# A rope table loaded one token group earlier: the order of groups in attention's last v part

## The chip, the core and the metric

The kernel runs on one core of a Trainium2 chip. The metric is the device time of one execution in microseconds (us). The engines named below are PE (TensorE, matrix products), DVE (VectorE), ACT (ScalarE), POOL (GpSimd) and SP, whose instruction queue issues the transfers. Each engine works through its own instructions strictly in order and waits on semaphores for the others.

## What is computed

One mixer layer over 1024 latent tokens with 256 context tokens in front, all in float32. A normalised and modulated input `h` (latent) or `hc` (context) goes through one wide projection. Branch A is a bidirectional chunked gated DeltaNet with 8 heads; branch B is differential softmax attention with 8 heads of two 64-wide halves. Both are gated, projected, merged and added to `x`. For the change only the preparation of branch B matters:

```
q_l = diff_heads(q_b, q_norm_w, rope)      # latent tokens: RMS norm of each 64, gain, 2-D rope
k_l = diff_heads(k_b, k_norm_w, rope)
k_c = diff_heads(k_bc, k_norm_w, None)     # context tokens: no rope, and no queries at all
v_l = v_b.reshape(...)                     # no norm, no rope
v_c = v_bc.reshape(...)
o_b = diff_attend(q_l, concat(k_c, k_l), concat(v_c, v_l), lam)
```

So keys and values are needed for 1024 + 256 tokens, queries for the 1024 latent ones only.

## The kernel before

Tokens lie in ten tiles of 128: tiles 0 to 7 are latent, 8 and 9 context. The modulated input `hs` stays on chip, transposed, each value split in two float32r numbers (high and low). It has three groups: tiles 0 to 3, 4 to 7, and the context's two tiles. The context's group lies in a pool of its own, in two buffers with the tags `s20` (high) and `s21` (low).

The attention projection is cut into ten **parts** of 256 columns: k 0 to 3, v 2 and 3, q 0 to 3 (v 0 and 1 were made earlier). `part_flow` takes a part's tokens in **groups** of two tiles, five groups for a k or v part (t0 = 0, 2, 4, 6, 8) and four for a q part. A group is 48 matmuls of 128x256 into one PSUM bank (`mm<-wh,hs` and `mm<-wl,hs`, recorded at L56, the helper that issues every matmul). `part_out` empties the bank. For v, ACT casts it (`vt`, L971), DVE takes the remainder (L972) and two transfers store both (`vd<-vt`, L976). For k and q, ACT copies (`raw`, L984) and squares (`sq`, L985), and `part_post` goes on: on DVE a sum of squares (L994, L995), then **the rope**, six products and sums that read the table (L1005, L1006, L1007, each twice); on PE four transposes (`tr<-ct,fin`, L63); a cast (ACT, `col`, L1025) and a remainder (DVE, L1026); two stores (L1031). The weights of the next part are loaded (`wr`, L888), cast by ACT (`wh`, L892) and their low halves made by POOL and DVE (`wl`, L893).

The rope table of the queries, 128 x 1024 floats with the norm's gain already in it, was written to memory (`tbd`) early on. There is no free room on chip for it, so it is put where the context's high half lies (tag `s20`, tile `hx`), once the last v part, the last work that reads context tokens, is through. That transfer is issued at L947, at the start of part q 0.

While this goes on, branch A's heads are prepared beside it: Gram products of keys (`gram`, PE), decay matrices (`X`, ACT, L1114 and L1116), a triangular inverse built from small blocks (`pz`, `p`, `pu` on PE, `ts` and `tmp` on DVE, L1165 and L1167; copies of `RR` into `X` and `t`, L1257, L1258, L1261).

Nothing of the order on the engines is written by hand. Each piece of work is a stream (a Python generator) that yields its next instruction with its engine, a planned duration and the planned ends of what it needs. `flow` always emits, over all streams, the instruction that could start earliest by its own running clocks of the engines and of the transfers, with a fixed bias per stream. So a shift in one stream changes which instruction is emitted next on every engine, until the streams fall back into step. `asides` is a stream that works off a list of small jobs.

Of the kernel before, what the change touches and what calls it, by code (L numbers as in the profile page):

```python
# [8 lines left out]
F32 = mybir.dt.float32  # L9
# [8 lines left out]
P = 128  # L18
D = 1024
KT = D // P  # L20
L = 1024
LC = 256
LT = L + LC
NT = LT // P
NL = L // P
# [9 lines left out]
PE, DVE, ACT, POOL, DMA, ADMA, DV2, PL1 = range(8)  # L35
# [8 lines left out]
class Block:  # L44
# [892 lines left out]
    def part_flow(self, parts):  # L937

        self.free, self.nb = [None, None], 0
        free = self.free  # L940
        for i, (kind, pair) in enumerate(parts):
            yield lambda: i in self.parts_
            hi, lo, tw = self.parts_.pop(i)
            if parts[i - 1][0] != kind == "q":
                self.hx = self.hc.tile([P, 2, L], F32, tag="s20", name="hx")
                self.rope["q"] = self.hx[:, 0].rearrange("p (a b t f) -> p a b t f", a=2, b=2, f=32), (
                    yield DMA, 1.5, [self.part_t[i - 1]], lambda: self.nc.sync.dma_start(self.hx[:, 0], self.tbd[0]))  # L947
            for t0 in range(0, NL if kind == "q" else NT, 2):
                yield lambda: len(free) > self.nb
                pt = self.pm.tile([P, 512], F32, tag="mm", name="mm")  # L950
                for j in range(2):
                    th, tl, o = self.hsel(t0 + j)
                    m = 0
                    for k in range(KT):
                        for ht, wt in ((th, hi), (th, lo), (tl, hi)):
                            t = yield PE, 0.1195, [free[self.nb], tw], lambda: self.mm(
                                pt[:, j * W:j * W + W], ht[:, k, o:o + P], wt[:, k], m == 0, m == 3 * KT - 1)
                            m += 1
                self.evacs.append(self.part_out(kind, pair, t0, pt, t, free, self.nb))
                self.nb += 1  # L960
            self.parts_done, self.part_t[i] = i + 1, t

    def part_out(self, kind, pair, t0, pt, t, free, n):

        nc, s, tk = self.nc, n % 2, self.tk
        yield lambda: self.posted[s] >= n // 2
        old = self.slot_t[s]
        if kind == "v":
            vt = [tk.tile([P, 2, W], F32R, tag=f"{x}{s}", name="vt") for x in ("ch", "cl")]
            pv = pt.rearrange("p (t c) -> p t c", t=2)  # L970
            t1 = yield ACT, 0.478, [t, old], lambda: nc.scalar.copy(vt[0], pv)  # L971
            t = yield DVE, 0.6, [t1, old], lambda: nc.vector.tensor_tensor(vt[1], pv, vt[0].bitcast(F32), ALU.subtract)  # L972
            free.append(t)
            self.slot_t[s] = []
            for i, x in enumerate((t1, t)):
                self.slot_t[s].append((yield DMA, 0.73, [x], lambda: nc.sync.dma_start(  # L976
                    self.vd[i, t0 * P:(t0 + 2) * P, pair * W:(pair + 1) * W].rearrange("(t p) c -> p t c", p=P),
                    vt[i].bitcast(F32))))
            self.posted[s] += 1
            return  # L980
        raw, sq = tk.tile([P, 2, 8, 32], F32, tag=f"raw{s}", name="raw"), tk.tile([P, 512], F32, tag=f"sq{s}", name="sq")
        v = pt.rearrange("p (g r h f) -> p h g r f", r=2, h=2, f=16)
        for hf in range(2):
            tr = yield ACT, 0.264, [t, old], lambda: nc.scalar.copy(raw[:, hf].rearrange("p g (r f) -> p g r f", r=2), v[:, hf])  # L984
        t = yield ACT, 0.478, [t, old], lambda: nc.scalar.activation(sq, pt, AF.Square)  # L985
        free.append(t)
        self.posts[s].append(self.part_post(kind, pair, t0, raw, sq, tr, t, s))

    def part_post(self, kind, pair, t0, raw, sq, tr, t, s):

        nc, tk, V, Q = self.nc, self.tk, self.nc.vector, self.nc.gpsimd
        g, (tb, tt) = self.rope["g"], self.rope[kind]
        ss = self.rsq[:, t0:t0 + 2, 4 * pair:4 * pair + 4] if kind == "q" else tk.tile([P, 2, 4], F32, tag=f"ss{s}", name="ss")
        t = yield DVE, 0.6, [t], lambda: V.tensor_reduce(ss, sq.rearrange("p (t g d) -> p t g d", t=2, d=64), AX.X, ALU.add)  # L994
        tw = yield DVE, 0.08, [t], lambda: V.tensor_scalar(ss, ss, 1.0 / 64, EPS, ALU.mult, ALU.add)  # L995
        tw = yield PL1, 1.65, [tw], lambda: self.power(ss, ss)
        fin = tk.tile([P, 2, 4, 64], F32, tag=f"fin{s}", name="fin")
        o = [fin[:, :, :, hf * 32:(hf + 1) * 32] for hf in range(2)]
        x = [raw[:, hf].rearrange("p (t g) f -> p t g f", g=4) for hf in range(2)]
        te = []  # L1000
        if t0 < NL:
            m = [sq[:, hf * W:hf * W + W].rearrange("p (t g f) -> p t g f", t=2, g=4) for hf in range(2)]
            T = lambda i, hf: tb[:, i, hf, t0:t0 + 2].unsqueeze(2).to_broadcast([P, 2, 4, 32])
            for hf in range(2):
                t1 = yield DV2, 0.35, [t, tr, tt], lambda: V.tensor_tensor(m[hf], x[1 - hf], T(1, 1 - hf), ALU.mult)  # L1005
                t2 = yield DV2, 0.35, [tr, tt], lambda: V.tensor_tensor(o[hf], x[hf], T(0, hf), ALU.mult)  # L1006
                te += [(yield DV2, 0.35, [t1, t2], lambda: V.tensor_tensor(o[hf], o[hf], m[hf],  # L1007
                                                                          (ALU.subtract, ALU.add)[hf]))]
        else:
            for hf in range(2):  # L1010
                te += [(yield DV2, 0.35, [tr], lambda: V.tensor_tensor(
                    o[hf], x[hf], g[:, hf].unsqueeze(1).unsqueeze(1).to_broadcast([P, 2, 4, 32]), ALU.mult))]
        if kind == "k":
            f8 = fin.rearrange("p t g d -> p (t g) d")
            te = [(yield POOL, 1.05, [te, tw], lambda: Q.tensor_tensor(
                f8, f8, ss.rearrange("p t g -> p (t g)").unsqueeze(2).to_broadcast([P, 8, 64]), ALU.mult))]
        yield self.psum()
        b = self.banks.pop(0)
        pt = self.gt_("tr")
        for j in range(2):  # L1020
            for i in range(2):
                t1 = yield PE, 0.109, [te, b], lambda: self.tr(pt[:, (2 * j + i) * P:(2 * j + i + 1) * P], fin[:, i, 2 * j:2 * j + 2, :].rearrange("p c f -> p (c f)"))
        col = [tk.tile([P, 2, W], F32R, tag=f"{y}{s}", name="col") for y in ("ch", "cl")]
        pv = pt.rearrange("p (j n) -> p j n", j=2)
        th = yield ACT, 0.478, [t1, self.slot_t[s]], lambda: nc.scalar.copy(col[0], pv)  # L1025
        tl = yield DVE, 0.6, [th, self.slot_t[s]], lambda: V.tensor_tensor(col[1], pv, col[0].bitcast(F32), ALU.subtract)  # L1026
        self.banks.append(tl)
        ends = []
        for i, y in enumerate((th, tl)):
            dst = (self.qd if kind == "q" else self.kd)[i, 2 * pair:2 * pair + 2, :, t0 * P:t0 * P + W]  # L1030
            ends.append((yield DMA, 0.73, [y], lambda: nc.sync.dma_start(dst.rearrange("j p n -> p j n"), col[i].bitcast(F32))))  # L1031
        self.slot_t[s] = ends
        self.posted[s] += 1
# [1189 lines left out]
```

## Time and profile before

| | us |
|---|---|
| three timed runs | 1928.17, 1931.37, 1931.5 |
| their median | 1931.37 |
| the profiled execution, its own time | 1929.92 |
| its span | 1927.8 |
| PE busy | 1885.5 (98% of the span) |
| DVE busy | 1446.3 (75%) |
| ACT busy | 1076.1 (56%) |
| POOL busy | 678.3 (35%) |

The time lies 2.1 us above the span. PE's granted clock is full in every slice but for rounding. PE stood still for 42 us of the span: 17 us in the first 50 us, 3 us between 50 and 587 us, 4 us between 587 and 700 us, and 18 us in all that follows. The stretch of this change lies between 587 us (the last v part starts) and 700 us (the second q part ends). "Idle before" in a row is how long the engine had stood still, with the instruction that released it.

### The profile page before, as it was taken

How to read it: one execution, taken by the hardware profiler on the slowest of the kernel's cores; microseconds unless marked ns; L12 is line 12 of the kernel's file. 1: busy time of each engine (PE TensorE's matmuls, PEld its weight loads, DVE VectorE, ACT ScalarE, POOL GpSimd, SP SyncE). 2: the span in 40 equal slices, each digit the busy share in tenths (PEclk: the TensorE clock that was granted, in tenths of full speed). 3: DMA queues.
4: the chain of work that ended last, by engine and by line, in shares of the span. 5: the costliest groups of instructions: out<-in, count | busy, mean ns of one | idle time of the engine just before them, and what ended most of it. 6: DMA issues, size and time to landing. Idle time of an engine off the chain costs nothing.

```text
span 1927.8 us, 37500 instructions
## 1 busy us (share of the span) xinstructions
PE 1885.5 (98%) x13807; PEld 1659.8 (86%) x13807; DVE 1446.3 (75%) x3613; ACT 1076.1 (56%) x2237; POOL 678.3 (35%) x610
## 2 busy tenths in 40 slices
PE   6999999999999999999999999999999999999999
PEld 4888888899999998888888888888997888888887
DVE  4697998957887887867865865338996979995677
ACT  4543444426233563677576656448885868884222
POOL 3200000005441342343333332326766667672203
PEclk9999999999999999999999999999999999999999
DMA  9144535575545557666785565666436474226542
GB/s 335 56 140 97 137 95 138 123 190 179 168 148 186 176 189 231 229 195 226 216 292 175 196 199 159 214 229 224 130 124 207 160 242 155 84 88 216 190 152 87
DMA packets 383039, 336.39 MB, mean 174 GB/s; under 512 B 142610, under 2 KB 323444, under 8 KB 381832
## 3 DMA queue, kind: packets, MB, share of 16 engines
q1 hardware_dynamic: 382855, 333.99, 55.2%
q8 instruction: 109, 1.79, 0.4%
q14 instruction: 75, 0.61, 0.1%
HBM read 222.14 MB, written 111.79 MB: 173 GB/s over the span
## 4 chain that ended last, share of the span: by engine, by line
PE 80%; DVE 7%; DMA 5%; ACT 4%; issue 2%; POOL 1%; SPq 1%; ACTq 0%; DVEq 0%; POOLq 0%
PE mm L56 40%; PE s L56 7%; PE v L56 5%; PE chain L56 5%; PE mb L56 5%; PE ma L56 4%; PE x L56 3%; PE t L63 3%; PE out L56 3%; PE gram L56 1%; DVE S L1579 1%; DMA sk<-gkq 1%; DVE ac L601 1%; PE tr L63 1%; PE mp L56 1%
## 5 line engine op out<-in xcount | busy, mean ns | idle before, releaser
L56 PE MATMUL mm<-hs,wh 128*128 128x512 f32 (+1 forms) x2048 | 648.6, 390 | 1.5 <-DVE hs L413 1.4
L56 PEld LDWEIGHTS mm<-hs,wh 128*128 128x128 f32 x2048 | 371.3, 189 | 58.9 <-DVE hs L413 1.9
L56 PE MATMUL mm<-hs,wl 128*128 128x512 f32 (+1 forms) x1024 | 397.6, 388 | 1.0 <-POOL wl L893 1.0
L56 PE MATMUL mm<-wh,hs 128*128 128x256 f32 (+1 forms) x1792 | 327.3, 283 | 0.3 <-ACT sq L985 0.3
L56 PEld LDWEIGHTS mm<-wh,hs 128*128 128x128 f32 x1792 | 276.8, 188 | 0.8 <-ACT sq L985 0.5
L1579 DVE TENSOR_SCALAR_CACHE_REDUCE S<-s,rsq 128x512 f32<-128x512 f32 (+1 forms) x384 | 239.5, 654 | 27.6 <-DMA vl<-vd 12.6
L56 PE MATMUL mm<-wl,hs 128*128 128x256 f32 (+1 forms) x896 | 253.3, 283 | 0.0
L1616 POOL TENSOR_TENSOR S<-S 128x1280 f32<-128x1280 f32 x64 | 189.1, 2958 | 91.9 <-ACT S L1609 90.6
L56 PEld LDWEIGHTS mm<-hs,wl 128*128 128x128 f32 x1024 | 193.9, 189 | 29.9 <-POOL wl L893 1.4
L1592 ACT ACTIVATE S<-S,mn 128x1280 f32<-128x1280 f32 x128 | 175.2, 1372 | 51.4 <-DVE mn L1591 51.3
L56 PEld LDWEIGHTS mm<-wl,hs 128*128 128x128 f32 x896 | 168.6, 188 | 0.1
L601 DVE SCALAR_TENSOR_TENSOR ac<-xc,convT,ac 128x1284 f32<-128x1284 f32 (+1 forms) x96 | 138.6, 1447 | 11.3 <-ACT ac L599 10.7
L56 PE MATMUL s<-kk,qh 128*128 128x512 f32 (+1 forms) x384 | 142.6, 372 | 1.9 <-DVE S L1579 1.7
L56 PE MATMUL s<-kk,ql 128*128 128x512 f32 (+1 forms) x384 | 133.0, 358 | 0.4 <-DMA ql<-qd 0.4
L1653 DVE TENSOR_TENSOR al<-t,ah 128x512 fp32r<-128x512 f32 (+1 forms) x192 | 106.8, 594 | 7.4 <-ACT ah L1648 6.0
L586 POOL MEMSET xc<- 128x2 f32 (+1 forms) x64 | 3.6, 101 | 297.3 <-ACT sq L635 113.8
L1167 DVE TENSOR_TENSOR ts<-ts,tmp 80x31 f32<-80x31 f32 (+15 forms) x248 | 92.2, 372 | 6.0
L1334 ACT ACTIVATE vd<-chain,edk 128x128 f32<-128x128 f32 x144 | 52.2, 370 | 76.9 <-PE chain L56 71.1
L56 PE MATMUL ma<-y,wh 128*128 128x512 f32 x256 | 93.0, 409 | 1.8 <-DVE g L1826 1.8
L1165 DVE TENSOR_TENSOR tmp<-ab,ts 80x31 f32<-80x31 f32 (+15 forms) x248 | 89.4, 360 | 6.4 <-DMA ab<-da 1.1
L1648 ACT CAST ah<-t 128x512 fp32r<-128x512 f32 (+1 forms) x192 | 88.1, 522 | 9.0 <-PE t L63 8.5
L56 PE MATMUL v<-al,vh 128*128 128x256 f32 x320 | 90.2, 282 | 0.7 <-DVE al L1653 0.6
(296 smaller groups left out, 4302.6 us busy)
## 6 DMA issues: line engine op xcount, KB each, us to landing
wr<-in_w_in_dram SPq DMA_DIRECT2D x48, 512.0 KB, 5.8
hx<-in_w_in_dram SPq DMA_DIRECT2D x64, 256.0 KB, 4.0
x<-xq SPq DMA_DIRECT2D x64, 256.0 KB, 4.8
X<-gcd SPq DMA_DIRECT2D x8, 1280.0 KB, 7.0
kd<-col SPq DMA_DIRECT2D x40, 256.0 KB, 2.1
xq<-X SPq DMA_DIRECT2D x16, 640.0 KB, 8.9
kk<-kd SPq DMA_DIRECT2D x16, 640.0 KB, 6.4
kq<-gkq SPq DMA_DIRECT2D x8, 1152.0 KB
```

Of the source, the lines that this page charges most:

```text
L56: self.nc.tensor.matmul(out, lhsT, rhs, start=start, stop=stop)
L63: self.nc.tensor.transpose(out, src, self.ident[:src.shape[0], :src.shape[0]])
L586: x["e"].append((yield PL1, 0.1, [old], lambda: nc.gpsimd.memset(xc[:, a:b], 0.0)))
L601: t = yield DV2, 1.21e-3 * wd, [t], lambda: nc.vector.scalar_tensor_tensor(ac[:, :wd], xc[:, j:j + wd], self.convw(j, x["ct"]), ac[:, :wd] ...
L1165: t = yield DV2, n * w / 960.0 + 0.08, [t if j else self.later(t, 2.5), t1], lambda: V.tensor_tensor(tv, ab[:, j + 1:, j:j + 1].to_broadca ...
L1167: t = yield DV2, n * w / 960.0 + 0.08, [t, t1], lambda: V.tensor_tensor(ts[:, j + 1:, :w], ts[:, j + 1:, :w], tv, ALU.subtract)
L1334: td = yield ACT, 0.251, [t], lambda: nc.scalar.activation(vd, pc[:, 1], AF.Copy, scale=self.edk[:, c, g:g + 1])
L1579: e = yield DVE, 0.675 if m == 512 else 0.408, [e, self.sfree[c].get(n - 4 + c)], lambda: self.nc.vector.tensor_scalar(x["S"][c][:, o:o + ...
L1592: x["x"].append((yield ACT, 1.36, [e], lambda: nc.scalar.activation(S, S, AF.Exp, bias=x["mn"][:, c:c + 1], scale=-1.0, accum_out=w["l0"][ ...
L1616: e = yield POOL, 2.9, [e], lambda: self.nc.gpsimd.tensor_tensor(S0, S0, S1, ALU.add)
L1648: e = yield ACT, 0.48 if nb == 4 else 0.27, [t, y["old", k]], lambda: self.nc.scalar.copy(y["ah", k][:, :, q], pv)
L1653: t = yield DVE, 0.603 if k < 2 else 0.322, [e, y["old", k]], lambda: self.nc.vector.tensor_tensor(y["al", k][:, :, q], pv, y["ah", k][:, ...
```

## The change

The last v part (the one whose successor is a q part) takes the context's group first and the latent groups after it. Right behind the context's group, a job for the table's transfer is put on the `asides` list; the transfer waits for the last matmul of that group only. `part_post` now asks that the table's transfer has been emitted before it starts for a query. No instruction is added or taken away in the planned work, and none changes its size.

```
-            if parts[i - 1][0] != kind == "q":
-                self.hx = self.hc.tile([P, 2, L], F32, tag="s20", name="hx")
-                self.rope["q"] = self.hx[:, 0].rearrange("p (a b t f) -> p a b t f", a=2, b=2, f=32), (
-                    yield DMA, 1.5, [self.part_t[i - 1]], lambda: self.nc.sync.dma_start(self.hx[:, 0], self.tbd[0]))
-            for t0 in range(0, NL if kind == "q" else NT, 2):
+            last = kind != "q" and parts[i + 1][0] == "q"
+            for t0 in (NL, *range(0, NL, 2)) if last else range(0, NL if kind == "q" else NT, 2):
...
                 self.nb += 1
+                if last and t0 == NL:
+                    self.asides.append(self.query_table(t))
             self.parts_done, self.part_t[i] = i + 1, t
+
+    def query_table(self, t):
+
+        self.hx = self.hc.tile([P, 2, L], F32, tag="s20", name="hx")
+        self.rope["q"] = self.hx[:, 0].rearrange("p (a b t f) -> p a b t f", a=2, b=2, f=32), (
+            yield DMA, 1.5, [t], lambda: self.nc.sync.dma_start(self.hx[:, 0], self.tbd[0]))
...
+        yield lambda: kind in self.rope
```

Line numbers behind the new function are six higher than before (five in `part_out`). What the change moves shows at three places. The first is SP's queue in the last two v parts; `vd<-vt` are the stores of v, `wr` the weights' loads, `X<-gcd` and `kq<-gkq` the loads of branch A's next head. Before:

```order
L1160 DMA ab<-da 80x1024
L888 DMA wr<-in_w_in_dram 128x4x256 x2
L976 DMA vd<-vt 128x2x256 x8
L1247 DMA xq<-X 128x5x256 x2
L976 DMA vd<-vt 128x2x256 x2
L1097 DMA X<-gcd 128x2x1280
L1104 DMA kq<-gkq 128x2304
L888 DMA wr<-in_w_in_dram 128x4x256 x2
L947 DMA hx<-tbd 128x1024
L976 DMA vd<-vt 128x2x256 x2
```

And after:

```order
L1166 DMA ab<-da 80x1024
L888 DMA wr<-in_w_in_dram 128x4x256 x2
L981 DMA vd<-vt 128x2x256 x4
L966 DMA hx<-tbd 128x1024
L981 DMA vd<-vt 128x2x256 x4
L1253 DMA xq<-X 128x5x256 x2
L981 DMA vd<-vt 128x2x256 x2
L1103 DMA X<-gcd 128x2x1280
L1110 DMA kq<-gkq 128x2304
```

The table's load moved from behind the three loads for branch A and the weights to behind the first four of twelve stores, the last two of which belong to the context's group.

The second place is PE around the first transposes of a query group. Before, 255 matmuls of the parts stand between the product `pu` of branch A's inverse and these transposes:

```order
L56 MATMUL mm<-wl,hs 128x256
L56 MATMUL mm<-wh,hs 128x256
L63 MATMUL tr<-ct,fin 128x128 x4
L56 MATMUL mm<-wh,hs 128x256
L56 MATMUL mm<-wl,hs 128x256
```

And after, 224:

```order
L56 MATMUL mm<-wh,hs 128x256 x2
L56 MATMUL mm<-wl,hs 128x256
L63 MATMUL tr<-ct,fin 128x128 x4
L56 MATMUL mm<-wh,hs 128x256 x2
L56 MATMUL mm<-wl,hs 128x256
```

They stand 31 matmuls earlier. The transposes of the next four query groups moved forward too, by 6, 6, 6 and 13 matmuls of the parts; from those of the sixth group on, PE's order is the old one.

The third place is DVE between the ropes of the fourth and of the fifth query group; `wl` makes a weight's low half, `RR` goes to `X` in copies of 32x320. Before, the piece behind the fourth rope ends so:

```order
L1187 TENSOR_SCALAR Z<-pz 128x320
L1257 COPY X<-RR 32x10x32
L1026 TENSOR_TENSOR col<-tr,col 128x512
L1134 TENSOR_TENSOR qk<-gram,X 128x256
L1137 SCALAR_TENSOR_TENSOR X<-gram,beta,X 128x128 x2
L1134 TENSOR_TENSOR qk<-gram,X 128x256
L1137 SCALAR_TENSOR_TENSOR X<-gram,beta,X 128x128
L893 TENSOR_TENSOR wl<-wr,wh 128x1024
L994 TENSOR_REDUCE rsq<-sq 128x2x4
```

And after:

```order
L1193 TENSOR_SCALAR Z<-pz 128x320
L1263 COPY X<-RR 32x10x32 x3
L1140 TENSOR_TENSOR qk<-gram,X 128x256
L1032 TENSOR_TENSOR col<-tr,col 128x512
L1143 SCALAR_TENSOR_TENSOR X<-gram,beta,X 128x128 x2
L1140 TENSOR_TENSOR qk<-gram,X 128x256
L1000 TENSOR_REDUCE rsq<-sq 128x2x4
```

Two more copies stand ahead of the fifth group's sum of squares (L1000); `wl` and one product `X` went behind its rope, and one `qk` ahead of the fourth rope. DVE's and ACT's orders are the old ones again behind the eighth query group, POOL's and SP's before that.

## The prediction

> **What bounds the kernel now.** I read the page's first part, then PE's busy time by stage, then the tile `hx` and the chain of waits around it. The page says what kind of kernel this is:
>
> ```profile
> span 1927.8 us, 37500 instructions
> PE 1885.5 (98%) x13807; PEld 1659.8 (86%) x13807; DVE 1446.3 (75%) x3613; ACT 1076.1 (56%) x2237; POOL 678.3 (35%) x610
> ```
>
> PE works nearly always. A change that adds and removes no matmul can only move the 42.3 us in which PE stood still. Busy times by stretch (length, then PE, PEld, DVE, ACT, POOL, granted clock, DMA share, GB/s) say where those are:
>
> ```profile
> 50.00:587.00 537.00, 534.17 (x3424) 482.50 (x3424) 434.34 (x767) 222.17 (x342) 87.82 (x125) 1.00 0.49 135
> 587.00:700.00 113.00, 108.80 (x1406) 105.98 (x1406) 93.56 (x233) 61.62 (x152) 33.40 (x32) 1.00 0.55 174
> 700.00:1927.80 1227.80, 1209.43 (x8740) 1049.90 (x8739) 894.38 (x2572) 769.64 (x1709) 539.89 (x426) 1.00 0.57 186
> ```
>
> In the stretch that the change touches PE stands still for 113.00 - 108.80 = 4.2 us. That is the ceiling of what can be won there. The chain of waits (start, length, what) shows the largest piece of it:
>
> ```profile
> 621.17 11.30 DMA hx<-tbd
> 632.49 0.42 DVE sq L1005
> ...
> 633.29 2.50 DVE fin L1007
> ...
> 636.49 0.43 DVE fin L1007
> ...
> 636.97 0.66 PE tr L63 x4
> ```
>
> The table is issued at 621.17, lands 11.30 us later, and the first rope runs from 632.49 to 636.92. In time order on PE:
>
> ```profile
> 634.83 0.28 PE L56 MATMUL mm<-wh,hs 128*128 128x256 f32 x1
> 636.97 0.66 PE L63 MATMUL tr<-ct,fin 128*128 128x128 f32 x4 [1.86 <-DVE fin L1007]
> ```
>
> Matmuls follow each other every 0.118 us (28.11 us for 239 below), so the transposes could have started at 634.95. PE lost 2.02 us by starts; 1.86 us is what the view prints.
>
> ```profile
> 564.13 28.11 PE mm L56 x239
> ```
>
> **The change, part by part.** First the load. SP's queue before (start, length of the issue), and ACT's cast for the group that is now the context's:
>
> ```profile
> 587.91 8.16 SPq L976 DMA_DIRECT2D vd<-vt  x4
> ...
> 618.18 1.19 SPq L1097 DMA_DIRECT2D X<-gcd  x1
> 619.41 0.46 SPq L1104 DMA_DIRECT2D kq<-gkq  x1
> 619.92 1.21 SPq L888 DMA_DIRECT2D wr<-in_w_in_dram  x2
> 621.17 3.31 SPq L947 DMA_DIRECT2D hx<-tbd  x1
> 593.65 0.59 ACT L971 CAST vt<-mm 128x512 fp32r<-128x512 f32 x1 [1.39 <-PE mm L56]
> ```
>
> The new place is behind the fourth of these stores, so at 587.91 + 8.16 = 596.07. PE has then been through the context's group for 2.4 us (ACT's cast of it starts at 593.65), so SP does not stand at the load. What is queued behind it are the next group's stores, whose casts come after 602. Around 596 the transfers are light; slices of 1.35 us from 586 on:
>
> ```profile
> GB/s 56 214 281 287 306 318 96 171 159 0 0 0 0 194 117 90 0 0 56 208 335 335 341 332 141 244 357 303 343 422 361 376 376 389 407 98 18 197 27 212
> ```
>
> The zeros are 598 to 603.6. My estimate is a landing by 601, and with the old 11.30 us it would be 607.4. The reader needs it at 628.7. The DMA wait of the rope is gone with 20 us to spare, and the load itself costs nothing. Its cover is the v part; without that cover it costs what it costs now. The 512 KB also leave the crowded slices up to 633, which can only help the weights behind which it stood.
>
> Five groups of v in another order are the same 240 matmuls, evacuations and stores. I put that at nothing.
>
> Now the first rope (group 0). DVE's rows for its sum of squares before, and an undisturbed rope further on (first and last of six):
>
> ```profile
> 627.85 0.69 DVE L994 TENSOR_REDUCE rsq<-sq 128x8 f32<-128x512 f32 x1 [2.73 <-ACT sq L985]
> 628.57 0.17 DVE L995 TENSOR_SCALAR rsq<-rsq 128x8 f32<-128x8 f32 x1
> ...
> 650.30 0.42 DVE L1005 TENSOR_TENSOR sq<-raw,hx 128x256 f32<-128x256 f32 x1
> ...
> 652.22 0.42 DVE L1007 TENSOR_TENSOR fin<-fin,sq 128x256 f32<-128x256 f32 x1
> ```
>
> An undisturbed rope takes 652.64 - 650.30 = 2.34 us, so with the table there it runs from 628.65 to 630.99. The transposes stand 31 matmuls earlier now: 634.95 - 31 x 0.1176 = 631.30. They find their input ready, 0.3 us in hand. **Term 1: -2.02 us** (-1.86 by the printed idle).
>
> One of the old rope's six instructions took 2.50 instead of 0.42 us, beside this one on POOL:
>
> ```profile
> 633.05 2.45 POOL L893 TENSOR_TENSOR wl<-wr,wh 128x1024 fp32r<-128x1024 f32 x1 [2.52 <-ACT wh L892]
> ```
>
> DVE's stall ends with POOL's instruction at 635.5; the stretched row is 2.08 us too long. The new rope is over 2 us before POOL starts, so this goes with the first wait. [...]
>
> Then the waits that come next. Group 2: its transposes were at 647.36, now 2.02 us and 6 matmuls (0.71) earlier: 644.63.
>
> ```profile
> 647.36 0.44 PE tr L63 x4
> 630.76 1.27 ACT L1116 ACTIVATE X<-X 128x1280 f32<-128x1280 f32 x1
> 634.77 1.04 ACT L892 CAST wh<-wr 128x1024 fp32r<-128x1024 f32 x1
> 642.03 0.61 ACT L985 ACTIVATE sq<-mm 128x512 f32<-128x512 f32 x1
> ```
>
> ACT was not waiting for PE there: it works through from 627.2. In the new order, from 632.87 on, it has a cast `col` 0.49, copies and square of group 1 1.01, `wh` 1.0, ten `X` 3.07 and their exponential 1.18 before the second `col`, which so ends at 640.2. DVE's `col`, `qk` and `X` (1.35) and the 3.13 us from sum to end of rope bring 644.7. **Term 2: +0.1 us**, between 0 and 0.6 (the next gap of ACT).
>
> Group 4 is where I see the main cost. Its rows before (DVE, POOL, PE's weight load):
>
> ```profile
> 655.03 1.53 DVE L1257 COPY X<-RR 32x320 f32<-32x320 f32 x1
> 658.89 1.22 DVE L893 TENSOR_TENSOR wl<-wr,wh 128x1024 fp32r<-128x1024 f32 x1
> 660.03 0.68 DVE L994 TENSOR_REDUCE rsq<-sq 128x8 f32<-128x512 f32 x1
> 662.74 0.42 DVE L1007 TENSOR_TENSOR fin<-fin,sq 128x256 f32<-128x256 f32 x1
> 654.01 2.37 POOL L893 TENSOR_TENSOR wl<-wr,wh 128x1024 fp32r<-128x1024 f32 x1 [1.79 <-ACT wh L892]
> 663.22 0.42 PEld L63 LDWEIGHTS tr<-ct,fin 128*128 128x128 f32 x4 [0.30 <-DVE fin L1007]
> ```
>
> DVE is full from the end of group 3's rope (652.64) to group 4's sum (660.03): 7.39 us. The new order takes out `wl` (1.14), a `qk` (0.44) and an `X` (0.26), and puts in two copies (0.34 each): 6.23 us. Group 3's rope starts when ACT has squared it, about 1.3 us earlier than before, and ends at 651.3. So group 4's rope ends at 651.3 + 6.23 + 3.13 = 660.7. PE's slot is 663.22 - 0.30 - 2.02 - 13 x 0.1176 + 0.1 = 659.5. PE waits 1.2 us where it waited 0.30. **Term 3: +0.9 us.** Its bounds are -0.30 (no wait) and +3.0 (POOL's low half lies over this rope as it did over the first, 2.08 more).
>
> Group 7's transposes waited too, behind two copies that are now made earlier:
>
> ```profile
> 678.52 0.64 DVE L1261 COPY t<-RR 32x160 f32<-32x160 f32 x2
> 683.97 0.66 PE L63 MATMUL tr<-ct,fin 128*128 128x128 f32 x4 [0.38 <-DVE Z L1228]
> ```
>
> DVE is 0.64 us lighter ahead of that rope. **Term 4: -0.38 us**, or 0.
>
> Behind group 7 all engines have their old order, and nothing there is fixed to a clock, so I let the shift run through to the end. **Sum: -2.02 + 0.1 + 0.9 - 0.38 = -1.4 us**, bounds -2.7 and -1.86 + 0.6 + 3.0 = +1.7. The profiled execution took 1929.92 us, so it becomes 1928.5. The four executions shown (1928.17, 1929.92, 1931.37, 1931.5) have their middle at 1930.65; the profiled one lies 0.7 below it. I predict 1930.65 - 1.4 = 1929.2 us.
>
> **Rivals.** A measurement of this kernel can tell about 0.2%, 3.9 us, from no change.
>
> *All waits go.* Group 2 and 4 find their ropes ready, and the 0.30 and 0.38 us go too: -2.7, and with the small waits around `pz` and group 8 about -3: 1927.6 us. For it speaks that DVE loses 3.75 us of idle and 2.08 us of stall; against it that DVE is full between 652 and 663.
>
> *The lock moves on (slower).* `wl` on POOL starts when the weights land and ACT has cast them. If that falls into group 4's rope, DVE loses 2.08 us where PE has nothing in hand: -1.4 + 2.08 = +0.7, 1931.3 us. It decides when POOL's `wl` starts between 655 and 660 in the new trace. Before, it started at 654.01 and stretched only a copy (1.53 us); the new weights are issued about 2 us earlier, which moves it away from the rope. [...]
>
> *The load does not get earlier.* If SP or the transfers held it until 632.49 as now, PE would meet the transposes 31 matmuls sooner and lose 3.65 us more: 1934.3 us. The zeros at 598 speak against it.
>
> *The shift is lost.* A later wait for a transfer that is not tied to PE eats it: 0, 1930.65 us. In 1227.80 us behind 700 PE is idle for 18.4 us in small pieces, so there is room for that, but I see no clock-bound one.
>
> **How the numbers follow.** Forecast 0.57, all waits go 0.18, shift lost 0.15, lock moves on 0.08, load not earlier 0.02. Each of the first four lies within 0.2%. For *faster* (below 1926.8 or so) I take a third of *all waits go*, plus the forecast with three timed runs whose spread before was 3.3 us: 0.10. For *slower* the load's case (0.02) and twice the lock: 0.04. Same: 0.86. Range: the sum's bounds around 1930.65 give 1927.9 to 1932.4; with the timed runs' scatter on the fast side, 1926.3 to 1932.5.
>
> **What the new profile would show.** Right: the load of `hx` issued at about 596 and landed before 605; no wait of L1011 (the rope's first line) for it; the first `tr<-ct,fin` at about 631.3 without idle time; the fifth with about 1 us idle behind `fin`; PE idle between 587 and 700 near 2.8 instead of 4.2 us. Wrong: the fifth transposes without a wait, or with 3 us beside a POOL `wl`; a `tr` that waits for a `hx` transfer; an end that has not moved although 700 us was reached 1.4 us earlier. A time outside 1926 to 1933 would mean that an order I take as unchanged behaves otherwise.

## The result, and the profile after

The change took 1926.99 us in the median of 22 runs (1923.9 to 1930.58), the kernel before 1929.73 us (1927.27 to 1936.1, 22 runs). The ratio is 0.9984, with a 95% interval from 0.9978 to 0.9991: a gain of 0.16%, inside the 0.2% that I had called no change, and inside the range. The forecast of 1929.2 us is 2.2 us too high: 0.9 of that lies in its starting point (1930.65 us, where 22 runs have their middle at 1929.73), the rest in the gain, 2.7 us where the sum was 1.4. Two more sets of runs gave 0.9986 [0.9977, 0.9995] and 0.9989 [0.9980, 0.9997]. Over all 44 timed runs of the change the mean is 1927.3 us, over 105 of the kernel before 1929.9 us: 2.6 us.

The first part of the page of the profiled execution of the change (its own time was 1926.13 us), then its busy times by stretch:

```profile
span 1924.0 us, 37505 instructions
PE 1883.2 (98%) x13807; PEld 1658.8 (86%) x13807; DVE 1445.1 (75%) x3613; ACT 1075.2 (56%) x2237; POOL 678.9 (35%) x610
```

```profile
50.00:587.00 537.00, 533.27 (x3419) 481.80 (x3419) 433.60 (x766) 220.90 (x342) 87.70 (x125) 1.00 0.49 135
587.00:700.00 113.00, 109.70 (x1417) 107.17 (x1416) 93.68 (x237) 62.68 (x155) 33.56 (x32) 1.00 0.56 178
700.00:1924.00 1224.00, 1207.16 (x8728) 1048.23 (x8726) 892.99 (x2570) 767.76 (x1705) 540.46 (x426) 1.00 0.57 186
```

In the stretch of the change PE now stands still for 3.3 us instead of 4.2. In two further profiles of the change it is 3.0 and 2.8 us, where 2.8 was predicted. The load, the first rope and the transposes after the change, each in time order on its engine:

```profile
587.68 8.61 SPq L981 DMA_DIRECT2D vd<-vt  x4
596.38 0.42 SPq L966 DMA_DIRECT2D hx<-tbd  x1
619.83 1.18 SPq L888 DMA_DIRECT2D wr<-in_w_in_dram  x2
```

```profile
628.82 0.42 DVE L1011 TENSOR_TENSOR sq<-raw,hx 128x256 f32<-128x256 f32 x1
...
630.74 0.42 DVE L1013 TENSOR_TENSOR fin<-fin,sq 128x256 f32<-128x256 f32 x1
```

```profile
631.35 0.28 PE L56 MATMUL mm<-wl,hs 128*128 128x256 f32 x1
631.47 0.60 PE L63 MATMUL tr<-ct,fin 128*128 128x128 f32 x4
```

The load is issued at 596.38, 24.8 us earlier. No view prints when it landed, but nothing waits for it: the rope's first line starts behind its own sum of squares, and the rope's last line ends at 631.16. The transposes start behind the matmul in front of them, with no idle time: the wait of 1.86 us is gone.

What PE waited for between 626 and 700 (us in total, times, longest), in the kernel before:

```profile
PE tr L63 <- DVE fin L1007: 2.1, 2, 1.9
PE tr L63 <- DVE Z L1228: 0.4, 1, 0.4
PE pz L56 <- issue: 0.2, 1, 0.2
```

And in the change, where these are the only two:

```profile
PE tr L63 <- DVE fin L1013: 1.1, 2, 0.8
PE tr L63 <- DVE Z L1234: 0.2, 1, 0.2
```

2.7 us have become 1.3. The longest that is left is at the fifth query group, 0.82 us, as the prediction had it in kind.

Behind 700 us the order of work is the old one, and I compare the starts of the same PE instruction (the n-th of 13807) in two traces. This is my own working, and I use it for all kernels below. "626 to 700" says by how much the kernel took longer over this piece than the profiled execution of the kernel before, "700 to 1900" the same behind it; the last column is the mean of the timed runs against the 1929.9 us.

| kernel | 626 to 700, us | 700 to 1900, us | ratio [95%] | mean of runs, us |
|---|---|---|---|---|
| before | 0 | 0 | | 0 |
| before, again | -0.4 | -0.9 | | |
| v order only | -0.5 | -1.4 | 0.9997 [0.9987, 1.0007] | -0.1 |
| no POOL half, q part 1 | -2.1 | -1.3 | 0.9994 [0.9985, 1.0003] | |
| the same again | -1.7 | -0.7 | 0.9996 [0.9987, 1.0004] | -1.3 (both) |
| early load, old order | -2.0 | +2.3 | 0.9994 [0.9985, 1.0002] | |
| the same again | -2.0 | +1.1 | 0.9985 [0.9975, 0.9995] | -1.4 (both) |
| change | -1.7 | -2.3 | 0.9984 [0.9978, 0.9991] | |
| change, second | -1.8 | -0.3 | 0.9986 [0.9977, 0.9995] | |
| change, third | -1.8 | +0.5 | 0.9989 [0.9980, 0.9997] | -2.6 (all) |
| change, load late | +5.8 | -1.3 | 1.0023 [1.0015, 1.0032] | +4.6 |
| change, no POOL half, q part 2 | -2.6 | -4.2 | 0.9984 [0.9975, 0.9993] | -3.6 |

The middle column is the reliable one: profiles of one program agree there within 0.4 us. In 700 to 1900 one kernel scatters by 2.8 us. Part of that has a place: ahead of branch A's product `chain` near 866 us PE waited for a transfer (`sk<-gkq`) for 1.6 and 1.8 us in the two profiles of the kernel before, and for 0, 1.8 and 1.7 us in the three of the change. The three profiles in the old order with both hindrances (the first three rows) average -0.3 over 626 to 700, the three of the change -1.75. So the change is worth 1.4 us there. That is the sum that was predicted, but not term by term (see below).

### The profile page after: what moved, and what is told of

It reads as the page before. It is cut to its first block, busy times and chain, and to the rows that moved or that the text cites. A ratio compares the mean times of both kernels' runs of the same rounds, so it can differ in the third digit from the quotient of the medians.

```text
span 1924.0 us, 37505 instructions
## 1 busy us (share of the span) xinstructions
PE 1883.2 (98%) x13807; PEld 1658.8 (86%) x13807; DVE 1445.1 (75%) x3613; ACT 1075.2 (56%) x2237; POOL 678.9 (35%) x610
## 4 chain that ended last, share of the span: by engine, by line
PE 56%; DVE 5%; ACT 2%; DMA 2%; issue 1%; POOL 1%; SPq 0%; ACTq 0%; DVEq 0%; POOLq 0%
PE mm L56 18%; PE s L56 7%; PE v L56 5%; PE chain L56 5%; PE mb L56 5%; PE ma L56 4%; PE x L56 3%; PE t L63 3%; PE out L56 3%; DVE S L1585 1%; PE gram L56 1%; DVE al L1659 1%; PE z L56 1%; DMA sk<-gkq 1%; ACT S L1598 0%
```

## The experiments

**The kernel before, once more**, for a second profile.

> The kernel before, once more, for its profile. PE stands still about 2 us at the first query transposes again (636.97 in the first profile), and reaches the cast behind the second q part (ACT, col, 699.62 us) within 0.4 us of then. The stretch from that cast to the end was 1228.2 us before and 1225.9 us with the change, although the order is the same there. If that 2.3 us is chance of one execution, it comes out anywhere between 1225 and 1230 here; if the change causes it, it stays at 1228.2 within 0.3 us.

It took 1931.03 us. The first ropes of its DVE and POOL and the first transposes, in time order:

```profile
634.35 0.43 DVE L1005 TENSOR_TENSOR sq<-raw,hx 128x256 f32<-128x256 f32 x1 [3.23 <-DMA hx<-tbd]
...
635.42 2.40 POOL L893 TENSOR_TENSOR wl<-wr,wh 128x1024 fp32r<-128x1024 f32 x1 [2.52 <-ACT wh L892]
635.48 2.61 DVE L1005 TENSOR_TENSOR sq<-raw,hx 128x256 f32<-128x256 f32 x1
...
638.95 0.66 PE L63 MATMUL tr<-ct,fin 128*128 128x128 f32 x4 [1.46 <-DVE fin L1007]
```

Here another of the rope's six instructions is the stretched one (the fourth, L1005, not the third, L1007), and again it is the one that starts beside POOL's `wl`. So the 2.1 us belong to POOL's instruction and not to a line of the rope, as the prediction had taken it from one pair of rows. In both profiles the stretched row ends 0.3 us behind POOL's (635.79 and 635.50; here 638.09 and 637.82). The recorded texts call this the lock; what the rows show is that one DVE instruction, 0.42 us long elsewhere, takes 2.50 and 2.61 us beside POOL's `wl`. PE waits 1.46 us, not 1.86: the size of the wait that the change removes differs by 0.4 us between executions of the same program. Behind 700 us, where the order of work is the same anyway, this execution was 0.9 us shorter than the first one, so a difference of that size there is chance.

**The order of the v groups alone.** The context's group first, the load where it was; all engines keep their old order but for the groups.

```
-            for t0 in range(0, NL if kind == "q" else NT, 2):
+            last = kind != "q" and parts[i + 1][0] == "q"
+            for t0 in (NL, *range(0, NL, 2)) if last else range(0, NL if kind == "q" else NT, 2):
```

> Only the order of the last v part's groups is changed (context first); the table is loaded where it was before, and all five engines have the order of before. Theory (the table's landing decides): no difference, ratio 1.000 within 0.0005, PE still 2 us idle at the first query transposes. Rival (the order of the v groups or of their stores is worth something by itself): ratio 0.9985.

Ratio 0.9997 [0.9987, 1.0007]. The rope waits 3.20 us for `hx<-tbd` and PE 1.45 us for the rope, as before. Five groups in another order cost nothing and gain nothing that these runs resolve, as the prediction put it.

**POOL's half away, the load late.** In the kernel before, the first half of `wl` that fell into the first rope (weights of q part 1) is made by DVE behind that rope. The plan's durations stay, so no order moves.

```
+            eng = nc.gpsimd if e == POOL and c0 != C_QB + W else nc.vector
-            ... lambda: (nc.gpsimd if e == POOL else nc.vector).tensor_tensor(
+            ... lambda: eng.tensor_tensor(
```

> The kernel before, with the low half of one weight (the one POOL made from 633.05 to 635.50 over the first rope) made by DVE right behind that rope instead; the table still lands late. Theory (the 2.50 us instruction in the first rope is POOL's lock, and the late table alone would have been just in time for the old place of the transposes): rope from 632.5 to 634.8 in 2.34 us, PE waits 0 to 0.2 us there instead of 1.9, about -1.9 us by 700 us, ratio 0.9990. Rival (the table's wait alone costs PE its 2 us): an instruction of 2.5 us stays, or PE still waits 2 us; ratio 1.000.

Its load, rope, `wl` and transposes, by tile and in time order:

```profile
L948 SPq DMA_DIRECT2D hx<-tbd x1: 3693/3693/3693, 621.5 to 621.5; - x1
```

```profile
632.61 0.43 DVE L1006 TENSOR_TENSOR sq<-raw,hx 128x256 f32<-128x256 f32 x1 [3.33 <-DMA hx<-tbd]
...
634.53 0.43 DVE L1008 TENSOR_TENSOR fin<-fin,sq 128x256 f32<-128x256 f32 x1
634.88 1.22 DVE L894 TENSOR_TENSOR wl<-wr,wh 128x1024 fp32r<-128x1024 f32 x1
...
635.54 0.60 PE L63 MATMUL tr<-ct,fin 128*128 128x128 f32 x4
```

The table is as late as ever, DVE waits 3.33 us for it, and PE waits for nothing: the rope ends at 634.96, the transposes start at 635.54 behind their matmul. The stretch is 1.7 to 2.1 us shorter, all of the first wait. A wait of 3.3 us for a transfer was harmless by itself, because the rope still ended 0.6 us ahead of PE's slot. In the second execution DVE waited 3.81 us, the rope ended at 635.93 and the transposes started at 635.99: still no wait, but with nothing to spare.

**The load early, POOL's half in place, the old order.** The context's group comes first, and the load is emitted behind the matmuls of the first latent group, which puts it at the same place of SP's queue as in the change (596.42); a job without an instruction stands where the load was planned, so that the plan does not move anything else.

```
-                    yield DMA, 1.5, [self.part_t[i - 1]], lambda: self.nc.sync.dma_start(self.hx[:, 0], self.tbd[0]))
+                    yield DMA, 1.5, [self.part_t[i - 1]], lambda: None)
...
+                if last and t0 == 0:
+                    self.hx = self.hc.tile([P, 2, L], F32, tag="s20", name="hx")
+                    self.nc.sync.dma_start(self.hx[:, 0], self.tbd[0])
```

> The context's group first and the table's load behind it, as in the change, but with the order of PE, DVE, ACT and POOL of before (only the load moves in SP's queue). Theory (the load does it, the new order of the engines costs 0.5 us at the fifth group): first rope ends at 631, PE's transposes start at 634.95 without a wait, the fifth group waits 0.3 us as before instead of 0.8, 700 us is reached 2.0 us earlier than before (the change: 1.6), ratio 0.9990 or, if what the change won behind 700 us is its own, 0.9980. Rival (the new order of instructions makes the gain, not the load): ratio 1.000.

```profile
629.37 0.42 DVE L1008 TENSOR_TENSOR sq<-raw,hx 128x256 f32<-128x256 f32 x1
...
631.29 0.42 DVE L1010 TENSOR_TENSOR fin<-fin,sq 128x256 f32<-128x256 f32 x1
633.77 2.40 POOL L893 TENSOR_TENSOR wl<-wr,wh 128x1024 fp32r<-128x1024 f32 x1 [2.48 <-ACT wh L892]
...
635.67 0.60 PE L63 MATMUL tr<-ct,fin 128*128 128x128 f32 x4
```

The rope is over 2.06 us before POOL starts, and 3.96 us before PE's slot. The stretch is 2.0 us shorter. So each cause alone is harmless here: the late table cost PE nothing without POOL's instruction beside the rope, and POOL's instruction nothing without the late table. Taking away either gives the whole gain in this stretch, and the change's new order on the engines is not needed for it. The whole time shows that less well: of the four sets of runs of these two kernels one lies clear of 1. In this stretch the change does on average 0.3 and 0.1 us *less* than the early load and the kernel with POOL's half on DVE, because its third and fifth groups wait longer: 0.24 and 0.82 us, against 0 and 0.29 in the early load.

**The change's order with the load late.** The load is issued behind the weights again, in the change's order.

```
-            yield DMA, 1.5, [t], lambda: self.nc.sync.dma_start(self.hx[:, 0], self.tbd[0]))
+            yield DMA, 1.5, [t], lambda: setattr(self, "late", lambda: self.nc.sync.dma_start(self.hx[:, 0], self.tbd[0])))
...
+        if c0 == C_QB + W:
+            self.late()
```

> The change's order on PE, DVE, ACT and POOL, but the table's load is issued where it stood before, behind the weights' loads at 621 us. This is the prediction's rival in which the load does not get earlier. Theory (the transposes stand 31 matmuls earlier, so the same late rope costs PE 3.65 us more than before): PE idle about 5.5 us at the first query transposes, 700 us reached 3.3 to 3.7 us later than before, ratio 1.0018. Rival (the order of the instructions makes the gain): ratio below 1.

Ratio 1.0023 [1.0015, 1.0032], 1934.54 us in the median. The first transposes on PE, and then its busy times by stretch (the last numbers of a row are the granted clock, the DMA share and GB/s):

```profile
637.12 1.09 PE L63 MATMUL tr<-ct,fin 128*128 128x128 f32 x4 [5.46 <-DVE fin L1015]
637.86 0.78 PE L56 MATMUL mm<-wh,hs 128*128 128x256 f32 x2
638.43 0.41 PE L56 MATMUL mm<-wl,hs 128*128 128x256 f32 x1
638.65 0.63 PE L56 MATMUL mm<-wh,hs 128*128 128x256 f32 x2
```

```profile
630.00:637.00 7.00, 1.66 (x15) 1.45 (x13) 4.30 (x6) 3.10 (x6) 3.06 (x2) 0.89 0.72 231
637.00:640.00 3.00, 2.88 (x14) 2.91 (x15) 0.69 (x1) 0.85 (x2) 0.00 (x0) 0.50 0.40 79
640.00:645.00 5.00, 5.00 (x35) 5.00 (x35) 3.98 (x9) 4.97 (x15) 1.74 (x1) 0.77 0.25 87
645.00:650.00 5.00, 5.00 (x46) 5.00 (x45) 2.40 (x7) 2.79 (x5) 0.00 (x0) 1.00 0.30 104
```

PE's wait is 5.46 us: 1.86 as before plus the 3.65 us of 31 pulled-forward slots makes 5.51. So the slots' price in the prediction's third rival is right for the idle time. But the stretch became 5.8 us longer than before, not 3.65. After the wait the granted clock is 0.50 and then 0.77 in the mean of five us; by PE's rows three matmuls take 0.64 us up to 642.27 and 0.35 us from 642.42 on. By these two rows of stretches PE lost 0.50 x 3.00 + 0.23 x 5.00 = 2.65 us more at most. By the starts of the same instructions, which stand in the same order in the change, it is 2.4 us, and later waits give a little back. The matmul `mm<-wl,hs` at 638.43 and the next one, three matmuls on, are 0.64 us apart, 0.21 each, against 0.118.

Full clock was back 5.2 us after work had begun. In two other profiles an idle of 2.1 to 2.2 us came before a lowered clock (0.69 and 0.78 in the mean of five us, see the last section).

**The change without POOL's half in the fourth to fifth group.** As above, for the weights of q part 2 (`c0 != C_QB + 2 * W`), in the change. The rows on DVE, POOL and PE around the fifth transposes, in the change:

```profile
652.70 2.37 POOL L893 TENSOR_TENSOR wl<-wr,wh 128x1024 fp32r<-128x1024 f32 x1 [2.12 <-ACT wh L892]
652.94 2.97 DVE L1263 COPY X<-RR 32x320 f32<-32x320 f32 x3
...
659.92 0.28 PE L56 MATMUL mm<-wl,hs 128*128 128x256 f32 x1
660.44 0.42 DVE L1013 TENSOR_TENSOR fin<-fin,sq 128x256 f32<-128x256 f32 x1
...
661.01 0.63 PE L63 MATMUL tr<-ct,fin 128*128 128x128 f32 x4 [0.82 <-DVE fin L1013]
```

> The change, with the low half of the next weight (POOL's from 652.70, beside which three copies on DVE took 2.97 instead of 1.0 us) made by DVE behind these copies instead. Theory (POOL's lock makes the fifth group's transposes late): the three copies take 1.0 us, DVE has 1.14 us more to do, so the fifth rope ends 0.8 us earlier and PE's wait of 0.8 us there goes; 0.8 us better than the change by 700 us, ratio 0.9987 within 0.0007. Rival (DVE is simply full there): the wait grows to 1.9 us, 1.1 us worse than the change.

And with that half on DVE, behind the three copies:

```profile
656.51 0.99 DVE L1264 COPY X<-RR 32x320 f32<-32x320 f32 x3
657.52 1.23 DVE L894 TENSOR_TENSOR wl<-wr,wh 128x1024 fp32r<-128x1024 f32 x1
...
663.74 0.63 PE L63 MATMUL tr<-ct,fin 128*128 128x128 f32 x4
```

The copies take 0.99 instead of 2.97 us; DVE makes the half in 1.23 us itself, less than the 1.98 us that it lost to it, and the fifth transposes do not wait. The stretch is 0.8 us shorter than in the change. The ratio is 0.9984 [0.9975, 0.9993], beside 0.9986 for the change on the same chip: a difference of 0.0002 that the intervals do not resolve. No version tried is shown to beat the change.

**The change a second time**, on the chip of the last two, and then the two that hold the old order **again beside the change**, for the question whether the change gains something behind 700 us that they don't.

> The change once more, with a second profile and more times. The first times gave 0.9984 (3.0 us), the profile 1.7 us between the first query group and 700 us and 2.3 us more behind it. Theory (1.7 us is the change, the rest behind 700 us is chance of the executions, as the profiles of the other kernels scatter there by -1.4 to +2.3 us): -1.7 us again by 700 us, any value within 2.5 us behind it, ratio 0.9991 within 0.0007. Rival (the change also saves 1 to 2 us behind 700 us): ratio 0.9984 within 0.0004 again, and the stretch behind 700 us shorter than before by 1 us or more again.

> The early load in the old order once more, beside the change on the same chip. Open is whether the change gains anything over it. Theory A: the two differ by the scatter between executions alone, since both take the two microseconds from the query part and differ there by 0.1 to 0.3 us; then this kernel and the change stand within 0.0007 of one another, both at 0.9985 to 0.9993 of the kernel before. Theory B: the order of the work in the change is worth some 1.5 us more behind 700 us; then this kernel stands at 0.9991 to 0.9995 and the change at 0.9983 to 0.9986.

> The change on the same chip as the early load in the old order. Theory A: within 0.0007 of that kernel. Theory B: 0.0007 to 0.0010 below it, 1.3 to 1.9 us.

> The kernel before with the first weight part's half on DVE, on the same chip. Theory A: within 0.0007 of the change. Theory B (the order of the change gains behind 700 us): 0.9991 to 0.9996, above the change by 0.0007 or more.

The early load in the old order came out at 0.9985, within 0.0004 of the change (0.9989), as theory A has it; the kernel with POOL's half on DVE at 0.9996, 0.0007 above the change, as theory B has it. With intervals of about 0.001 to either side, neither decides between the two. Over all runs the two stand at -1.3 and -1.4 us and the change at -2.6. The early load has a step of its own that the others lack, in both its executions: PE waits for a transfer of branch A's scan near 921 us. Its rows, of the first and of the second profile:

```profile
920.37 0.68 PE L56 MATMUL chain<-S,sk 128*128 128x128 f32 x4 [1.73 <-DMA sk<-gkq]
```

```profile
924.36 0.68 PE L56 MATMUL chain<-S,sk 128*128 128x128 f32 x4 [1.85 <-DMA sk<-gkq]
```

So the early load loses up to 1.9 us of idle there (2.4 us by the starts, in both profiles) by a transfer that meets its reader late. Why it does so in this kernel alone was not tested. For the kernel with POOL's half on DVE the profiles show no such place.

## Why the prediction was right, and where its sizes were off

The mechanism stands: the table's load moved, the first wait went, and a smaller one appeared at the fifth group. The sum for the stretch is the measured one, -1.4 predicted and -1.75 + 0.3 = -1.4 by the starts on PE, but that they agree to a tenth is luck, since the sizes of its terms were off both ways. All sizes below are by starts: a transpose's start less that of the matmul in front of it and 0.118 us.

*The load* was to be issued at 596.07 and to cost nothing: 596.38, no wait for it anywhere, and SP's next store starts at 603.00, as soon as the cast that it stores has ended (602.39 and 0.6 us). Shown.

*Term 1, -2.02 us.* Shown: no idle at the first transposes, which start at 631.47 (predicted 631.30). That the stretched instruction goes with the wait is shown by the early load in the old order and by POOL's half taken away. What the prediction did not see is that the two causes covered for each other, so that either cure would have been enough. And the size was that of one execution: two others in the old order waited 1.46 and 1.45 us, 0.4 less.

*Term 2, +0.1 us.* It is 0.4 us at the third group (0.24 us of printed idle), within its bounds. Part of the miss is a reading: 647.36 came from the chain, which counts from the end of the matmul in front, while the transposes started at 647.20, so PE's slot was earlier than was reckoned. The row before, and then in the change:

```profile
647.20 0.60 PE L63 MATMUL tr<-ct,fin 128*128 128x128 f32 x4
```

```profile
644.99 0.63 PE L63 MATMUL tr<-ct,fin 128*128 128x128 f32 x4 [0.24 <-DVE fin L1013]
```

*Term 3, +0.9 us.* It is +0.7. The place was right. The 0.30 us that was set off against the new wait is the idle of the weight load's row; PE's own rows before are these:

```profile
662.85 0.28 PE L56 MATMUL mm<-wh,hs 128*128 128x256 f32 x1
663.22 0.66 PE L63 MATMUL tr<-ct,fin 128*128 128x128 f32 x4
```

PE lost 663.22 - 662.85 - 0.118 = 0.25 us there before, and 661.01 - 659.92 - 0.118 = 0.97 in the change. The rope ended at 660.86 where 660.7 was predicted, by errors that cancel: the fourth group's rope ended 0.3 us earlier than predicted (651.01), and DVE's piece behind it took 6.7 us instead of 6.23. In that piece the prediction had 1.53 us for the old copy and 0.34 for each of the two new ones, 2.2 us; the three took 2.97 beside POOL's `wl`, instead of the 0.99 of the last experiment. The prediction knew that this `wl` falls on a copy, and argued only that it would miss the rope, which it did. PE's slot came 0.5 us later than predicted (660.04 for 659.5).

*Term 4, -0.38 us.* Half: by the two lists of waits above, 0.4 us behind `Z` at L1228 became 0.2 at L1234. So it is -0.2, not all of it.

With the measured sizes the four terms make -2.02 + 0.4 + 0.7 - 0.2 = -1.1 us. The profiled execution of the change gained 1.7 us over the one before, so 0.6 us more went in small waits that the sum left out, the one ahead of `pz` among them (0.2 us in the first list, gone in the second). Against the mean of the old order, in which term 1 is 0.3 smaller, 1.7 becomes 1.4.

*Behind 700 us* the prediction let the shift run through unchanged. By the timed runs the change gained 2.6 us, 1.2 more than the stretch. The three profiles of the change and the three of the old order with both hindrances differ by 2.7 us in the mean as well, and there the rest lies *ahead* of the change: -1.3 us up to 560, where PE has the same instructions in the same order, 0.0 from 560 to 626, -1.4 from 626 to 700, and 0.0 behind that, with single values from -2.3 to +0.5. So in these executions the rest is most likely chance. For the timed runs that is not shown. Set against what their stretch says (counted from the old order's -0.3), the change is 1.1 us better in the timed runs, the change with the late load 1.5 and that without POOL's half 1.4, while the three kernels in the old order are 0.1 to 0.3 us worse. Whether the new order gains this by something that the profiles don't hold, or how much of it is chance, stays open.

*The rivals.* POOL's instruction did not move on into a rope (its `wl` started at 652.70, ahead of the 655 from which it was to decide), but the copies ahead of that rope took 2.97 us beside it, and that cost 0.8 us all the same, as the experiment without it shows. Not all waits went: 1.3 us of them are left. The time came out near that rival's 1927.6 us nonetheless, by a gain outside this stretch that no rival explains. The load that does not get earlier was built and is slower by more than was priced: 5.8 us in the stretch instead of 3.65, by the granted clock of 0.50 behind PE's wait. The shift was not lost.

## What to carry to other kernels

When two late causes lie one behind the other (here a table and POOL's instruction beside the rope), the waits on the profile's chain add up, but the slack of the reader counts once: removing either can give everything, so price the smaller edit too. Freeing a buffer earlier by taking its last reader first cost nothing here, where the pieces are equal, but an emission order that pulls PE's next instructions forward by n slots raises the price of every late input by n slots (31 of them here, the wait from 1.86 to 5.46 us), and in the run with the late load by about 2.4 us more, with the granted clock at 0.50 behind that wait. A gain of 0.1% needs the starts of the same instruction in two traces to be seen at its place; the whole time scattered here by more than the gain from one execution to the next.

## What the runs showed of the hardware

Behind PE's idle of 5.46 us in the change with the late load the granted clock was 0.50 up to 5.2 us after work had begun, which cost about 2.4 us more. A shorter idle came before a lowered clock too. In two of the twelve profiles PE stood still for over 2 us near 598, in front of the small products of branch A's inverse. The row in the change without POOL's half, then the rows of its busy times from 595 on:

```profile
599.17 0.21 PE L56 MATMUL p<-Z,RR 32*32 32x32 f32 x1 [2.14 <-issue]
```

```profile
595.00:600.00 5.00, 2.86 (x133) 2.57 (x132) 2.31 (x4) 2.58 (x5) 2.85 (x5) 0.97 0.67 213
600.00:605.00 5.00, 5.00 (x33) 5.00 (x32) 4.38 (x12) 2.76 (x9) 0.00 (x0) 0.69 0.14 52
605.00:610.00 5.00, 5.00 (x109) 4.61 (x108) 4.64 (x13) 1.89 (x5) 1.45 (x4) 1.00 0.30 105
```

The clock fell to 0.69 in the mean of 5 us (for 3.4 us by the first two rows, if it was 0.50 wherever it was not full), and between 560 and 626 this execution took 2.3 us longer than the kernel before, the idle included; the second profile of the early load shows the same (2.20 us idle, 0.78, and 2.26 us). In the profiles of the kernel before, the change and the first one of the early load the same product waited 0.47, 0.88 and 0.88 us, and the clock was 1.00 from 595 to 605. In the other seven it was 1.00 in the mean from 587 to 700, but for the late load, with 1.00 from 590 to 630. Of the 83 runs of the kernel before that were timed beside the experiments, the 20 with a mean granted clock below 1.00 took 2.1 us longer in the mean than the 63 at 1.00. No trace shows where their clock fell. If it is this, it makes about a fifth of the variance between these 83 runs (0.24 x 0.76 x 2.1 squared is 0.8, of 3.7), so most of the scatter has other causes.

Beside POOL's `wl` of 2.4 us one DVE instruction of the first rope, 0.42 us long elsewhere, took 2.50, 2.61, 2.63 and 2.44 us in four profiles (the kernel before, the same again, the v order only, the change with the load late), each time until 0.3 us behind the end of POOL's. In the change three copies `X<-RR` took 2.97 us beside a `wl`, and 0.99 us in the kernel in which DVE made that half. Not all instructions of DVE did so: in the change `col` took its 0.69 us at 633.65 beside the `wl` that ran from 633.21 to 635.61.
